# An encoder block on one core: matrix N turned on ACT, outputs at the chain's priority, paired value products, held-back filler, routing order

## The chip, the cores and the metric

One core of a Trainium2 chip runs the whole kernel. The metric is the device time of one execution in microseconds; lower is better. The engines are TensorE (PE, with its weight loads as PEld), VectorE (DVE), ScalarE (ACT), GpSimd (POOL) and SyncE (SP, which issues most transfers).

## The reference

One layer over 2048 tokens of width 1024, in float32. Two token mixers run in parallel on the same normalised input, and a routed channel mixer follows:

```python
h = rms_norm(x, norm_mix_g)
u = h @ w_in                                  # RWKV columns | q, k, v | two gates
y_rwkv = rwkv7_bidir(token_shift(u[..., :RWKV_COLS]), ...)
y_attn = banded_gqa_attention(q, k_att, v_att, attn_sink)   # blocks of 128, window 128
merged = sigmoid(gl_rwkv) * (y_rwkv @ w_proj_rwkv) + sigmoid(gl_attn) * (y_attn @ w_proj_attn)
x = x + merged @ w_out
x = x + expert_choice_moe(rms_norm(x, norm_ffn_g), ...)     # 16 experts take their 256 best tokens each
return rms_norm(x, norm_final_g)

# the RWKV scan, once forwards and once backwards, 8 heads of 64:
s_kk = S @ kk_t
S = S * w_t - outer(s_kk, a_t * kk_t) + outer(v_t, k_t)
y_t = S @ r_t
```

The attention has 8 query heads on 2 key-value heads of 64. The router takes softmax(h @ w_router) and the 256 largest affinities for each expert.

## The kernel before, in words

The kernel runs in stages. First come the normalisation and the RWKV input products (to about 400 us). Then a **prep** (to about 945): 32 iterations of `Prep` build from keys, decays and rates the chunked form of the scan, 64 chunks of C = 32 tokens, with the products for the two gates ("gates", L500, `mm<-h,w`) as filler on TensorE. The chunked form needs, for each chunk and head, the inverse of a triangular 32 x 32 matrix N. `Invert` makes it: it loads N for one direction and one quarter of the sequence, 128 matrices at a time with one matrix in each partition, and solves row after row on DVE: L410 multiplies rows of X by a column of N into `tmp`, L411 sums them. There are eight inversions, three inside the prep and five (`late`) at the start of and inside the next stage, four rows a step.

The **chain** (945 to 1770) is the recurrence: 64 steps, each for both directions (`Chain.step`). A step issues for each direction the products with W (L659, `ps<-W,PRA`), a copy `ur` on ACT, the products with X (L666), four copies into W on ACT (L672), the state products (L679, `ps<-W,KT`) with DVE's scaling (L682) into the next W, and the outputs (L687, `y<-W,PRA`). `Steps` runs the two directions in these four parts, n = 0 to 3. A scheduler turns the program into an order for each engine: an instruction written inside `high_priority(offset=...)` is placed as if it had been written that much earlier, and `issue_after(i)` keeps what is inside behind instruction i. Parts n = 0 to 2 run at the chain's priority, and part n = 3, the outputs, doesn't. Between the parts `fill` issues gates (`GATE_STEP` = 4, 6, 4, 0 of them behind part 0, 1, 2, 3). The attention (`attention`, a generator) is cut into pieces which are issued between steps: scores (L757, L758), softmax, transposes of the probabilities (L789) and the value products (L796), two a key block, one for each key-value head, in different halves of the array. After each four steps a block's outputs are added up into `yacc` (L861) and `finish_rwkv` normalises them (L701 to L711), turns them (L714) and stores them.

**Stage 3** (1792 to 2187) projects, gates, multiplies by w_out (`pm`), and makes for each of 16 token tiles the normalised row h2, the routing logits `plg`, the softmax `aff` (`softmax16`) and `z` (L1096, the tile's row for the output). The **routing** (to 2266) turns the affinities over (`aT`, L1143) and finds each expert's threshold by 30 rounds of counting on DVE (L1162), one for each bit, with small matmuls on TensorE; in the rounds DVE also does `rem` (L1157) for splitting the affinities into parts `r5`, and pieces of the splitting of the first experts' weights (L1314, called `small`). ACT meanwhile copies the first three experts' slices of weights (L1308) and the first part of the affinities (L1154, `r<-aff`). The **experts** (to 3411) fill TensorE.

Of the kernel before, what the change touches and what calls it, by code (L numbers as in the profile page):

```python
# [9 lines left out]
F32 = mybir.dt.float32  # L10
# [3 lines left out]
AF = mybir.ActivationFunctionType  # L14
ALU = mybir.AluOpType
# [4 lines left out]
D = 1024  # L20
# [3 lines left out]
NBLK = T // 128  # L24
HEADS = 8
NPAIR = 4
C = 32
NSTEP = T // C
# [22 lines left out]
GATE_PREP, GATE_STEP = 5, (4, 6, 4, 0)  # L51
# [331 lines left out]
class Invert:  # L383


    def __init__(self, k, d, q):
        self.k, self.d, self.q = k, d, q
        self.i = 0

    def run(self, n):  # L390
        k, d, q, nc = self.k, self.d, self.q, self.k.nc
        if self.i > C:
            return
        if self.i == 0:
            self.N = k.inv.tile([128, C, C], F32, name="N")
            for p in range(NPAIR):
                for e in range(2):
                    r0 = (3 - 2 * e - p % 2) * 32
                    nc.sync.dma_start(self.N[(2 * p + e) * 16:(2 * p + e) * 16 + 16],
                                      k.pra[q][r0:r0 + 32, d, p, e, :, 0:C].rearrange("s u t -> u s t"))  # L400
            self.X = k.inv.tile([128, C, C], F32, name="X")
            self.tmp = k.inv.tile([128, C, C], F32, name="tmp")
            nc.gpsimd.memset(self.X, 0.0)
            nc.gpsimd.memset(self.X.rearrange("p s t -> p (s t)")[:, 0:C * C:C + 1], 1.0)
            self.i = 1
        X, N, tmp = self.X, self.N, self.tmp
        for i in range(self.i, min(C, self.i + n)):
            t, r = (i, slice(0, i)) if d == 0 else (C - 1 - i, slice(C - i, C))
            col = N[:, r, t]
            nc.vector.tensor_mul(tmp[:, :i, :i], X[:, r, r], col[:, None, :].to_broadcast([128, i, i]))  # L410
            nc.vector.tensor_reduce(out=X[:, r, t], in_=tmp[:, :i, :i], op=ALU.add, axis=AX.X)  # L411
        self.i = min(C, self.i + n)
        if self.i == C:
            nc.sync.dma_start(k.xt[d][q].rearrange("p h u s t -> (p h u) s t"), X)
            self.i = C + 1
# [309 lines left out]
def attention(k, b):  # L725
# [3 lines left out]
    nc = k.nc  # L729
    q, bq = divmod(b, 4)  # L730
    lo, hi = max(0, b - 1), min(NBLK, b + 2)
    nk = hi - lo
# [4 lines left out]
    for h in range(2):  # L737
        r = slice(h * 64, h * 64 + 64)
# [42 lines left out]
            nc.vector.tensor_scalar(t, t, den[:, i:i + 1], None, op0=ALU.mult)  # L781
        yield 1
    av = k.ps_a.tile([128, 4, 128], F32, name="pa")
    for c in range(nk):
        pT = k.att.tile([128, 2, 4, 128], F32, name="pT", bufs=3)
        for kv in range(2):
            pt = k.ps_a.tile([128, 4, 128], F32, name="pa")
            for i in range(4):
                nc.tensor.transpose(pt[:, i], sc[kv * 4 + i][:, c * 128:(c + 1) * 128], k.ident)  # L789
            if kv:  # L790
                nc.vector.tensor_copy(pT[:, kv], pt)
            else:
                nc.scalar.activation(pT[:, kv], pt, AF.Copy)
        for kv in range(2):
            rows = slice(kv * 64, kv * 64 + 64)
            nc.tensor.matmul(av[rows], lhsT=vs[:, c, rows], rhs=pT[:, kv], start=(c == 0),  # L796
                             stop=(c == nk - 1), tile_position=(0, kv * 64))
        if c < nk - 1:
            yield 1
    ya = k.att.tile([128, 4, 128], F32, name="yat")  # L800
    nc.scalar.activation(ya, av, AF.Copy)
# [3 lines left out]
class Steps:  # L805
# [17 lines left out]
    def step(self, s, fill):  # L823
        k, nc, tc = self.k, self.k.nc, self.k.tc
        i, j = divmod(s, 4)
        blk = [i, NBLK - 1 - i]
        if j == 0:
            self.y = [k.ps_y.tile([128, NPAIR, 2, 64], F32, name=f"y{d}") for d in range(2)]
            if i >= NBLK // 2:
                self.old = []  # L830
                for d in range(2):
                    self.old.append(k.ln.tile([128, 512], F32, name="yold", bufs=2))
                    nc.sync.dma_start(self.old[d], k.ypart[blk[d]])
        if j % 2 == 0:
            for d in range(2):
                with tc.high_priority(offset=k.chain_lead):
                    self.ch[d].load(2 * i + j // 2 + 1)
        steps = [self.ch[d].step(s, self.y[d]) for d in range(2)]
        for n in range(4):
            with ExitStack() as es:  # L840
                if n < 3:
                    es.enter_context(tc.high_priority(offset=k.chain_lead))
                first, second = self.order, 1 - self.order
                mark = next(steps[first])
                with tc.issue_after(mark):
                    mark = next(steps[second])
            if n < 3:
                self.order = second
            fill(n, mark)
        if j < 3:  # L850
            return
        for d in range(2):
            src = self.y[d].rearrange("p c e i -> p (c e i)")
            acc = self.yp.tile([128, 512], F32, name="yacc")
            if i < NBLK // 2:
                with tc.high_priority(offset=k.chain_lead):
                    nc.scalar.activation(acc, src, AF.Copy)
                nc.scalar.dma_start(k.ypart[blk[d]], acc)
            else:
                with tc.high_priority(offset=k.chain_lead):  # L860
                    nc.vector.tensor_add(acc, src, self.old[d])  # L861
                with tc.high_priority(offset=500):
                    finish_rwkv(k, blk[d], acc)


def token_mixers(k, gates, el):
# [4 lines left out]
    with ExitStack() as es:  # L871
# [121 lines left out]
                    break  # L993

        def between(n, mark):
            gates.run(GATE_STEP[n], after=mark)

        gates.run(GATE_MID)
        for s in range(NSTEP):
# [9 lines left out]
def stage3(k, out):  # L1009
# [3 lines left out]
    with ExitStack() as es:  # L1013
# [11 lines left out]
        for b in ORDER:  # L1025
# [36 lines left out]
            for tt in range(4):  # L1062
# [25 lines left out]
                pl = ps_l.tile([128, NEXP], F32, name="plg")  # L1088
                for i in range(KD):
                    nc.tensor.matmul(pl, lhsT=hT[:, i], rhs=wr[:, i], start=(i == 0), stop=(i == KD - 1))  # L1090
                k.last_exp, last = softmax16(k, xp, pl, k.aff[:, tid], rs)
                nc.scalar.activation(h2, xg, AF.Copy, scale=rs)
                nc.sync.dma_start(k.h2[t0:t0 + 128], h2)
                z = xp.tile([128, D], F32, name="z")
                with tc.issue_after(last):
                    nc.vector.scalar_tensor_tensor(out=z, in0=x, scalar=rs, in1=gz, op0=ALU.mult, op1=ALU.mult)  # L1096
                nc.sync.dma_start(out[t0:t0 + 128], z)


def softmax16(k, pool, lg, out, rs):  # L1100
# [6 lines left out]
    e = pool.tile([128, NEXP], F32, name="sme")  # L1107
    ex = nc.scalar.activation(e, lg, AF.Exp, bias=m, scale=rs, accum_out=s)
    nc.vector.reciprocal(s, s)
    return ex.ins, nc.vector.tensor_scalar(out, e, s, None, op0=ALU.mult).ins  # L1110


def route_constants(k, pool):
# [14 lines left out]
def route(k, rp, small):  # L1128
# [7 lines left out]
    with ExitStack() as e2:  # L1136
# [24 lines left out]
        for bit in range(29, -1, -1):  # L1161
            count = nc.vector.tensor_scalar(junk, aTf, cand.bitcast(F32)[:, 0:1], None, op0=ALU.is_ge, op1=ALU.add,  # L1162
                                            accum_out=cnt)
            with tc.issue_after(count.ins):
                if bit in rest:
                    rest[bit]()
                else:
                    next(small, 0)
# [38 lines left out]
def stage4(k, out):  # L1207
# [3 lines left out]
    with ExitStack() as es:  # L1211
# [117 lines left out]
        xs_n = xt.tile([128, 2, KD, CAP], F32R, name="xs")  # L1329
        for h in range(2):  # L1330
            turn(nxt[2], xs_n, h)
        for _ in small:
            pass
        prev = None
        for n in range(N + 1):
            e, f = divmod(n, KD)
# [221 lines left out]
```

## Time and profile before

| | us |
|---|---|
| median of three runs | 3417.12 (3413.95 to 3420.2) |
| profiled execution, its own time | 3421.18 |
| its span | 3419.2 |
| PE busy in the span | 3115.1 (91%) |
| DVE busy | 2330.7 (68%) |
| ACT busy | 1472.7 (43%) |

The mean granted clock of TensorE is 0.955 of full speed. The busy share is an average over stages: TensorE has hardly a gap in the input products, stage 3 and the experts, and gaps in the prep, the chain and the routing, which is where the change works. All times within the program are microseconds from the start of the span.

### The profile page before, as it was taken

The page shows a single profiled execution, that of the slowest core. Times are in us where ns is not written, and L with a number is a line of the kernel's source. Part 1 is how long each engine was busy: PE and PEld are TensorE (multiplying, and loading weights), DVE is VectorE, ACT ScalarE, POOL GpSimd, SP SyncE. Part 2 cuts the span into 40 slices and gives each one's busy share as a digit, 9 for nine tenths or more (in the row PEclk, how much of TensorE's full clock was granted, in tenths as well). Part 3 has the DMA queues.
Part 4 walks back from the last instruction along what each step waited for, and adds up shares of the span by engine and source line. Part 5 has one row for each costly group of instructions (what it writes and reads, how often), then busy time and mean ns, then how long its engine had stood idle before and what let it go on. Part 6 is the DMA issues. An engine that isn't in the chain of part 4 may idle for free. (4 is left out here: it accounts for less than half of the span.)

```text
span 3419.2 us, 65351 instructions
## 1 busy us (share of the span) xinstructions
PE 3115.1 (91%) x26062; PEld 2575.6 (75%) x26062; DVE 2330.7 (68%) x4902; ACT 1472.7 (43%) x2828; POOL 286.7 (8%) x457
## 2 busy tenths in 40 slices
PE   7999898889878888988969999669999999999998
PEld 6888786667656565565647888559999999999997
DVE  6434679798868887776766666466666666666665
ACT  5111455545425454455553333324444444444443
POOL 0000000000020100010100000001112111121111
PEclk9999899999989998999979999879999999999999
DMA  4212587878787667677766554436666666666663
GB/s 147 83 74 90 179 250 219 250 207 247 215 198 182 165 164 174 169 180 191 201 192 207 197 203 161 148 141 223 229 227 247 244 236 232 224 248 245 234 234 124
DMA packets 464576, 665.16 MB, mean 195 GB/s; under 512 B 162312, under 2 KB 345480, under 8 KB 445968
## 3 DMA queue, kind: packets, MB, share of 16 engines
q1 hardware_dynamic: 387824, 535.14, 51.0%
q10 hardware_dynamic: 58304, 59.79, 5.4%
q0 software_dynamic: 18144, 66.07, 5.1%
q8 instruction: 205, 3.36, 0.4%
q14 instruction: 99, 0.81, 0.1%
HBM read 483.66 MB, written 177.21 MB: 193 GB/s over the span
## 5 line engine op out<-in xcount | busy, mean ns | idle before, releaser
L500 PE MATMUL mm<-h,w 128*128 128x512 f32 x2112 | 619.4, 425 | 28.4 <-ACT ev L524 10.0
L91 PE MATMUL pg<-xs,wg 128*128 128x256 f32 x2048 | 583.6, 285 | 0.0
L92 PE MATMUL pg<-xs,wg 128*128 128x256 f32 x2048 | 582.0, 284 | 0.0
L93 PE MATMUL pg<-xs,wg 128*128 128x256 f32 x2048 | 579.6, 283 | 0.0
L500 PEld LDWEIGHTS mm<-h,w 128*128 128x128 f32 x2112 | 385.6, 197 | 122.0 <-ACT ev L524 11.9
L92 PEld LDWEIGHTS pg<-xs,wg 128*128 128x128 f32 x2048 | 392.4, 192 | 4.6 <-DVE xs L1264 0.2
L91 PEld LDWEIGHTS pg<-xs,wg 128*128 128x128 f32 x2048 | 392.3, 192 | 4.6 <-ACT xs L1263 0.2
L93 PEld LDWEIGHTS pg<-xs,wg 128*128 128x128 f32 x2048 | 392.3, 192 | 0.0
L98 DVE TENSOR_TENSOR wg<-raw,wg 128x2048 fp32r<-128x2048 f32 x125 | 286.3, 2290 | 106.7 <-ACT wg L97 106.5
L97 ACT ACTIVATE w<-wraw 128x1024 fp32r<-128x1024 f32 x135 | 142.6, 1058 | 293.7 <-issue 155.2
L1351 ACT ACTIVATE sg<-pg 128x256 f32<-128x256 f32 x128 | 49.3, 385 | 488.3 <-PE pg L93 486.2
L97 ACT ACTIVATE wg<-raw 128x2048 fp32r<-128x2048 f32 x125 | 238.8, 1910 | 0.1
L410 DVE TENSOR_TENSOR tmp<-X,N 128x1 f32<-128x1 f32 (+30 forms) x248 | 189.2, 763 | 36.9 <-DMA N<-pra 21.1
L83 PE MATMUL mm<-h,w 128*128 128x512 f32 x480 | 189.6, 396 | 20.3 <-ACT w L97 13.0
L92 PE MATMUL py<-wd,hd 128*128 128x512 f32 x512 | 203.1, 397 | 0.0
L91 PE MATMUL py<-wd,hd 128*128 128x512 f32 x512 | 201.0, 393 | 0.0
L93 PE MATMUL py<-wd,hd 128*128 128x512 f32 x512 | 198.4, 390 | 0.0
L98 DVE TENSOR_TENSOR w<-wraw,w 128x1024 fp32r<-128x1024 f32 x135 | 164.7, 1221 | 45.3 <-ACT w L97 44.7
L84 PE MATMUL mm<-h,w 128*128 128x512 f32 x480 | 188.7, 394 | 0.0
L85 PE MATMUL mm<-h,w 128*128 128x512 f32 x480 | 188.4, 393 | 0.0
L1352 DVE TENSOR_TENSOR sg<-pg,sg 128x256 f32<-128x256 f32 x128 | 54.2, 423 | 193.0 <-ACT sg L1351 193.0
L672 ACT ACTIVATE W<-ps 32x128 f32<-32x128 f32 x512 | 137.5, 269 | 70.5 <-PE ps L666 53.1
(302 smaller groups left out, 6243.8 us busy)
## 6 DMA issues: line engine op xcount, KB each, us to landing
raw<-w_exp SPq DMA_DIRECT2D x128, 1536.0 KB, 6.6
wraw<-w_in SPq DMA_DIRECT2D x103, 512.0 KB, 5.1
PRA<-pra SPq DMA_DIRECT2D x64, 512.0 KB, 5.9
pra<-PR SPq DMA_DIRECT2D x64, 256.0 KB, 4.7
pra<-A SPq DMA_DIRECT2D x64, 256.0 KB, 3.8
kt<-KT ACTq DMA_DIRECT2D x128, 128.0 KB, 5.1
gl<-ev ACTq DMA_DIRECT2D x64, 256.0 KB, 4.0
KT<-kt SPq DMA_DIRECT2D x128, 128.0 KB, 5.9
```

What stands on the lines that cost most here:

```text
L83: nc.tensor.matmul(ps, lhsT=w[:, 0, i], rhs=hs[i][:, 0], start=(i == 0), stop=False)
L84: nc.tensor.matmul(ps, lhsT=w[:, 0, i], rhs=hs[i][:, 1], start=False, stop=False)
L85: nc.tensor.matmul(ps, lhsT=w[:, 1, i], rhs=hs[i][:, 0], start=False, stop=(i == KD - 1))
L91: nc.tensor.matmul(out, lhsT=w[0], rhs=x[0], start=start, stop=False)
L92: nc.tensor.matmul(out, lhsT=w[0], rhs=x[1], start=False, stop=False)
L93: return nc.tensor.matmul(out, lhsT=w[1], rhs=x[0], start=False, stop=stop)
L97: nc.scalar.activation(hi, x, AF.Copy)
L98: (eng or nc.vector).tensor_sub(lo, x, hi)
L410: nc.vector.tensor_mul(tmp[:, :i, :i], X[:, r, r], col[:, None, :].to_broadcast([128, i, i]))
L500: nc.tensor.matmul(self.ps, lhsT=w[:, t // 2, i], rhs=h[:, t % 2], start=(self.i == 0), stop=(self.i == 3 * KD - 1))
L672: nc.scalar.activation(W[qd(u), o, e].rearrange("p g i -> p (g i)"), ps[qd(u), 128:256], AF.Copy)
L1352: nc.vector.tensor_mul(sg, pg[:, 1], sg)
```

## The change

Five edits, independent of each other in the code:

```diff
 class Invert:
...
             self.N = k.inv.tile([128, C, C], F32, name="N")
+            self.tmp = k.inv.tile([128, C, C], F32, name="tmp")
...
-                    nc.sync.dma_start(self.N[(2 * p + e) * 16:(2 * p + e) * 16 + 16],
+                    nc.sync.dma_start(self.tmp[(2 * p + e) * 16:(2 * p + e) * 16 + 16],
...
             self.X = k.inv.tile([128, C, C], F32, name="X")
-            self.tmp = k.inv.tile([128, C, C], F32, name="tmp")
+            nc.scalar.activation(self.N, self.tmp.rearrange("p s t -> p t s"), AF.Copy)
...
-            col = N[:, r, t]
+            col = N[:, t, r]
```

N is loaded into `tmp`, ACT copies it transposed into N, and L410 reads a row of that in place of a column.

```diff
     av = k.ps_a.tile([128, 4, 128], F32, name="pa")
-    for c in range(nk):
-        pT = k.att.tile([128, 2, 4, 128], F32, name="pT", bufs=3)
...
-        for kv in range(2):
-            rows = slice(kv * 64, kv * 64 + 64)
-            nc.tensor.matmul(av[rows], lhsT=vs[:, c, rows], rhs=pT[:, kv], start=(c == 0),
-                             stop=(c == nk - 1), tile_position=(0, kv * 64))
-        if c < nk - 1:
+    pTs = []
+    for c in range(nk + 1):
+        if c < nk:
+            pT = k.att.tile([128, 2, 4, 128], F32, name="pT", bufs=3)
...
+            pTs.append(pT)
+        if c:
+            with k.tc.issue_after(mm.ins):
+                for kv in range(2):
+                    rows = slice(kv * 64, kv * 64 + 64)
+                    nc.tensor.matmul(av[rows], lhsT=vs[:, c - 1, rows], rhs=pTs[c - 1][:, kv], start=(c == 1),
+                                     stop=(c == nk), tile_position=(0, kv * 64))
+        if c < nk:
             yield 1
```

The value products of a key block are issued one piece later, behind the next block's transposes.

```diff
             with ExitStack() as es:
-                if n < 3:
-                    es.enter_context(tc.high_priority(offset=k.chain_lead))
+                es.enter_context(tc.high_priority(offset=k.chain_lead))
...
-                with tc.high_priority(offset=500):
+                with tc.high_priority(offset=500 if i + 1 < NBLK else -400):
                     finish_rwkv(k, blk[d], acc)
...
         def between(n, mark):
-            gates.run(GATE_STEP[n], after=mark)
+            gates.run(GATE_STEP[n] if s < NSTEP - 8 else GATE_STEP[n] // 2, after=mark)
```

The outputs get the chain's priority too; in the last eight steps half as many gates are issued (what is left is issued behind the last step), and the last blocks' finishes are placed later.

```diff
-                k.last_exp, last = softmax16(k, xp, pl, k.aff[:, tid], rs)
-                nc.scalar.activation(h2, xg, AF.Copy, scale=rs)
+                k.last_exp = softmax16(k, xp, pl, k.aff[:, tid], rs)
+                with tc.issue_after(k.last_exp):
+                    nc.scalar.activation(h2, xg, AF.Copy, scale=rs)
                 nc.sync.dma_start(k.h2[t0:t0 + 128], h2)
-                z = xp.tile([128, D], F32, name="z")
-                with tc.issue_after(last):
-                    nc.vector.scalar_tensor_tensor(out=z, in0=x, scalar=rs, in1=gz, op0=ALU.mult, op1=ALU.mult)
+                z = xp.tile([128, D], F32, name="z", bufs=2)
+                nc.vector.scalar_tensor_tensor(out=z, in0=x, scalar=rs, in1=gz, op0=ALU.mult, op1=ALU.mult)
...
+            k.last_count = count.ins
...
-        for _ in small:
-            pass
+        with tc.issue_after(k.last_count):
+            for _ in small:
+                pass
```

`z` gets a second buffer and no longer stands behind the softmax, and the pieces of weight splitting that are left over stay behind the last count.

What the scheduler makes of it, at three places. On TensorE in the chain's 37th step of the kernel before, from the last outputs ahead of the state products on. The names with W_8662 are the second direction's, those with W_8640 the first's; 8 state products of each, and outputs of the first behind six gates:

```order
L687 MATMUL y_14759<-W_8662,PRA_14396 32x64 x3
L789 MATMUL pa<-ident,sc 128x128
L687 MATMUL y_14759<-W_8662,PRA_14396 32x64
L789 MATMUL pa<-ident,sc 128x128
L679 MATMUL ps_14788<-W_8640,KT_8644 64x64 x8
L679 MATMUL ps_14799<-W_8662,KT_8666 64x64 x8
L500 MATMUL mm<-h,w 128x512 x6
L687 MATMUL y_14758<-W_8640,PRA_14384 32x64
L789 MATMUL pa<-ident,sc 128x128 x4
```

The same step of the kernel after (W_8665 is the second direction, W_8643 the first):

```order
L689 MATMUL y_14767<-W_8665,PRA_14404 32x64 x8
L689 MATMUL y_14766<-W_8643,PRA_14392 32x64
L681 MATMUL ps_14796<-W_8643,KT_8647 64x64 x8
L681 MATMUL ps_14807<-W_8665,KT_8669 64x64 x3
L689 MATMUL y_14766<-W_8643,PRA_14392 32x64
L681 MATMUL ps_14807<-W_8665,KT_8669 64x64
L689 MATMUL y_14766<-W_8643,PRA_14392 32x64
L681 MATMUL ps_14807<-W_8665,KT_8669 64x64
```

The last state products of the second direction now alternate with outputs of the first, and this alternation goes on to the last state product, with the gates behind it.

On DVE at the start of the routing, before, from the last tile's affinities on:

```order
L1110 TENSOR_SCALAR aff<-sme,sms 128x16
L1096 SCALAR_TENSOR_TENSOR z<-x_22657,rs_22732,gz 128x1024
L1314 TENSOR_TENSOR wg<-raw,wg 128x256 x4
L1314 TENSOR_TENSOR wd<-raw,wd 128x256 x4
L1143 COPY aT<-pr 128x256
L1149 MEMSET cand 128x1
L1162 TENSOR_SCALAR junk,cnt<-aT,cand 128x256
```

And after:

```order
L1102 SCALAR_TENSOR_TENSOR z<-x_22665,rs_22740,gz 128x1024
L1115 RECIPROCAL sms<-sms 128x1
L1116 TENSOR_SCALAR aff<-sme,sms 128x16
L1150 COPY aT<-pr 128x256
L1156 MEMSET cand 128x1
L1169 TENSOR_SCALAR junk,cnt<-aT,cand 128x256
L1322 TENSOR_TENSOR wg<-raw,wg 128x256
```

z has moved ahead of the affinities, and the eight pieces that stood ahead of aT stand behind the last count now.

On ACT at the same place, before, from the last tile's exponentials on:

```order
L1108 ACTIVATE sme,sms<-plg,smx,rs_22732 128x16
L1308 ACTIVATE wg<-raw 128x2048
L1308 ACTIVATE wd<-raw 128x1024
L1154 ACTIVATE r_22835<-aff 128x256
L1308 ACTIVATE wg<-raw 128x2048
L1308 ACTIVATE wd<-raw 128x1024
```

And after:

```order
L1114 ACTIVATE sme,sms<-plg,smx,rs_22740 128x16
L1099 ACTIVATE h_22736<-xg,rs_22740 128x1024
L1316 ACTIVATE wg<-raw 128x2048
L1316 ACTIVATE wd<-raw 128x1024
L1316 ACTIVATE wg<-raw 128x2048
L1316 ACTIVATE wd<-raw 128x1024
L1316 ACTIVATE wg<-raw 128x2048
L1316 ACTIVATE wd<-raw 128x1024
L1161 ACTIVATE r_22843<-aff 128x256
```

The copy of the affinities has moved from behind the first pair of weight copies to behind the third.

## Rows read from the trace of the kernel before

**Rows 1.** Windows by stage: busy us (instructions) of each engine.

```profile
core 0: us, PE busy (x) PEld busy (x) DVE busy (x) ACT busy (x) POOL busy (x), PEclk, DMA share, GB/s
...
400.00:945.00 545.00, 493.29 (x4083) 392.94 (x4082) 462.99 (x921) 290.03 (x640) 5.17 (x8) 0.95 0.77 228
945.00:1770.00 825.00, 707.86 (x9959) 475.66 (x9957) 629.03 (x1547) 407.60 (x1194) 91.48 (x282) 0.93 0.72 177
```

**Rows 2.** Windows inside the prep and at the start of the chain.

```profile
545.00:655.00 110.00, 89.05 (x677) 71.31 (x678) 103.79 (x198) 60.69 (x133) 1.12 (x2) 0.88 0.76 229
655.00:698.00 43.00, 40.79 (x357) 31.63 (x355) 30.08 (x71) 17.15 (x37) 0.00 (x0) 1.00 0.79 226
698.00:754.00 56.00, 47.67 (x392) 38.36 (x391) 55.49 (x103) 27.74 (x61) 0.00 (x0) 0.91 0.72 213
...
829.00:930.00 101.00, 84.97 (x653) 65.02 (x654) 97.82 (x177) 49.42 (x110) 0.09 (x1) 0.92 0.72 213
945.00:1004.00 59.00, 39.47 (x415) 28.43 (x414) 47.57 (x82) 13.81 (x35) 15.98 (x42) 0.83 0.83 198
```

**Rows 3.** Groups of instructions by line, DVE: busy, mean ns, idle before.

```profile
L410 DVE TENSOR_TENSOR tmp<-X,N 128x1 f32<-128x1 f32 (+30 forms) x248 | 189.2, 763 | 36.9 <-DMA N<-pra 21.1 <-DMA kr<-kT 5.1 <-DMA pra<-PR 4.4
```

**Rows 4.** Groups by line and form, DVE, 545 to 946 us.

```profile
L98 DVE TENSOR_TENSOR w<-wraw,w 128x1024 fp32r<-128x1024 f32 x33 | 40.2, 1222 | 7.2 <-ACT w L97 7.2
...
L333 DVE TENSOR_TENSOR PR<-krv,G 128x256 f32<-128x256 f32 x44 | 18.1, 422 | 0.0
...
L410 DVE TENSOR_TENSOR tmp<-X,N 128x961 f32<-128x961 f32 x3 | 5.6, 1862 | 0.0
...
L410 DVE TENSOR_TENSOR tmp<-X,N 128x256 f32<-128x256 f32 x3 | 1.9, 619 | 0.0
```

**Rows 5.** The page's costliest groups: an ACT copy of 1024 elements.

```profile
L97 ACT ACTIVATE w<-wraw 128x1024 fp32r<-128x1024 f32 x135 | 142.6, 1058 | 293.7 <-issue 155.2
```

**Rows 6.** State products (L679): ns min/median/max, first and last start.

```profile
L679 PE MATMUL ps<-W,KT x2016: 219/222/369, 975.8 to 1756.5; 128*64 128x64 f32 x184
```

**Rows 7.** Timeline of PE in the chain: start us, us, engine, line.

```profile
1396.73 1.02 PE L796 MATMUL pa<-pT,vs 128*64 128x512 f32 x2
...
1401.02 2.10 PE L500 MATMUL mm<-h,w 128*128 128x512 f32 x8
...
1462.96 0.43 PE L687 MATMUL y<-W,PRA 128*32 128x64 f32 x16
1463.32 1.15 PE L679 MATMUL ps<-W,KT 128*64 128x64 f32 x32
...
1668.93 1.15 PE L679 MATMUL ps<-W,KT 128*64 128x64 f32 x32
1670.01 0.31 PE L687 MATMUL y<-W,PRA 128*32 128x64 f32 x6
```

**Rows 8.** Timeline of PE between the chain and stage 3.

```profile
1767.11 1.08 PE L796 MATMUL pa<-pT,vs 128*64 128x512 f32 x4
...
1783.47 1.08 PE L714 MATMUL pa<-ident,yacc 128*128 128x128 f32 x4 [13.81 <-DVE yacc L711]
1791.18 1.09 PE L714 MATMUL pa<-ident,yacc 128*128 128x128 f32 x4 [6.63 <-DVE yacc L711]
```

**Rows 9.** Timeline of DVE at the start of the routing.

```profile
2195.58 0.23 DVE L1110 TENSOR_SCALAR aff<-sme,sms 128x16 f32<-128x16 f32 x1
2206.02 1.28 DVE L1096 SCALAR_TENSOR_TENSOR z<-x,rs,gz 128x1024 f32<-128x1024 f32 x1 [10.20 <-DMA out<-z]
2207.22 1.42 DVE L1314 TENSOR_TENSOR wg<-raw,wg 128x256 fp32r<-128x256 f32 x4
...
2209.90 0.42 DVE L1143 COPY aT<-pr 128x256 f32<-128x256 f32 x1
...
2213.08 0.44 DVE L1157 TENSOR_TENSOR rem<-aff,r 128x256 f32<-128x256 f32 x1
```

**Rows 10.** Timeline of ACT at the start of the routing.

```profile
2198.00 0.90 ACT L1154 ACTIVATE r<-aff 128x256 bf16<-128x256 f32 x1
...
2206.55 1.04 ACT L1308 ACTIVATE wd<-raw 128x1024 fp32r<-128x1024 f32 x1
```

More of the change, by code (lines that the diff above doesn't have):

```diff
@@ L783, in attention @@
     av = k.ps_a.tile([128, 4, 128], F32, name="pa")
-    for c in range(nk):
-        pT = k.att.tile([128, 2, 4, 128], F32, name="pT", bufs=3)
-        for kv in range(2):
[L787 to L794, printed above, removed]
-            rows = slice(kv * 64, kv * 64 + 64)
-            nc.tensor.matmul(av[rows], lhsT=vs[:, c, rows], rhs=pT[:, kv], start=(c == 0),
-                             stop=(c == nk - 1), tile_position=(0, kv * 64))
-        if c < nk - 1:
+    pTs = []
[3 more added lines that the diff above has]
+            for kv in range(2):
+                pt = k.ps_a.tile([128, 4, 128], F32, name="pa")
+                for i in range(4):
+                    mm = nc.tensor.transpose(pt[:, i], sc[kv * 4 + i][:, c * 128:(c + 1) * 128], k.ident)
+                if kv:
+                    nc.vector.tensor_copy(pT[:, kv], pt)
+                else:
+                    nc.scalar.activation(pT[:, kv], pt, AF.Copy)
+            pTs.append(pT)
+        if c:
+            with k.tc.issue_after(mm.ins):
+                for kv in range(2):
+                    rows = slice(kv * 64, kv * 64 + 64)
+                    nc.tensor.matmul(av[rows], lhsT=vs[:, c - 1, rows], rhs=pTs[c - 1][:, kv], start=(c == 1),
+                                     stop=(c == nk), tile_position=(0, kv * 64))
+        if c < nk:
             yield 1
@@ L1109, in softmax16 @@
     nc.vector.reciprocal(s, s)
-    return ex.ins, nc.vector.tensor_scalar(out, e, s, None, op0=ALU.mult).ins
+    nc.vector.tensor_scalar(out, e, s, None, op0=ALU.mult)
+    return ex.ins
 def route_constants(k, pool):
```

## Prediction

> **What bounds the kernel now.** I read the busy time by stage first [rows 1]. TensorE is full in the input products, in stage 3 and in the experts; nothing here touches those. In the prep (400 to 945 us) it is busy 493 of 545 us, in the chain (945 to 1770) 708 of 825, so an edit there is worth what it takes out of TensorE's gaps or out of the recurrence, and what it adds to either.
>
> The prep in stretches [rows 2]: between two inversions (655 to 698) TensorE is busy 40.8 of 43 us. In the three stretches with an inversion it idles 110 − 89.0 = 21.0, 56 − 47.7 = 8.3 and 101 − 85.0 = 16.0 us, while DVE is busy 94, 99 and 97%: there DVE sets the pace. The same at the start of the chain (945 to 1004, fourth inversion): TensorE idles 19.5 of 59 us.
>
> In the chain a step takes 12.6 us: the state products (L679) of 63 steps start between 975.8 and 1756.4 us, 62 intervals [rows 6]. It is a recurrence (PRA products, copy, X products, four copies a direction, state products, scaling), so what TensorE puts in front of the last state product counts whole.
>
> **Invert: N turned round on ACT.** The strided multiplication takes 1862 ns for 961 elements and 619 for 256: 1.76 ns an element and 168 fixed [rows 4]. The nearest contiguous multiplication of DVE with two operands, L333, takes 422 ns for 256, and L98 1222 for 1024: 1.04 an element [rows 4]. An inversion multiplies the sum of i² for i up to 31 = 10,416 elements, so 0.72 ns each is 7.5 us, of L410's 189.2 / 8 = 23.7 us [rows 3]; eight give 60 us of DVE. This holds if the stride is the cause. The bounds are 0 and 60.
>
> The Trainium skill, SBUF — State Buffer, Specifications, says SBUF has 16-byte lines and that an access that crosses to a new one pays a penalty; N was read at 128 bytes' stride, and the matched pair of 256 elements, 619 against 422 ns, agrees. [...]
>
> Where it lands: three inversions in the prep save 22.5 us of DVE in stretches where TensorE idles 45; PE, ACT and DMA take over some of it: I take −19 (bounds −10 and −25). At the start of the chain −4 of 7.5, since the load of N is waited for there too. In the chain the four that are left (30 us of DVE) stand in DVE's order beside the scaling that each step waits for; most of it lies beside TensorE's own work: −5 (bounds 0 and −12). The copy costs ACT 1.06 us a time [rows 5], eight times, strided perhaps twice that; in the chain it stands in ACT's order between ur and the W copies, so it is on the recurrence, and it now waits for the load where DVE waited before (21.1 us in three waits, [rows 3]): +2 (bounds 0 and +10). Sum of the edit: **−26**.
>
> **Outputs at the chain's priority.** The listing of the order shows what happens: outputs (L687, 32-column tiles) slide in between the second direction's state products (L679, 64-column tiles), in the most frequent pattern one output ahead of the last state product, in others up to seven one by one; 140 returns over the chain. All changes of tile shape on TensorE go from 675 to 921, those between outputs and state products from 59 to 404. Price: 16 outputs start at 1462.96 and end 0.43 later [rows 7]; one takes 0.22, as a state product does at its shortest [rows 6], so the last starts at 1463.17, and the state products begin at 1463.32: 0.15 us later. The other way: 32 state products from 1668.93, 1.15 long, last start 1669.86, next output 1670.01: 0.15 [rows 7]. In a run the 32 are 0.93 / 31 = 0.03 apart. So a change costs 0.12, 246 more of them **+30 us**, nearly all before the last state product. Bounds: below, 0.12 with half hidden behind the waits for W copies, +15; above, a whole product of 0.22 drained at each of two changes a return, 140 × 0.44 = +62. I take 30.
>
> The Trainium skill, TensorEngine Tiling (Array Packing), Key Properties, says that changing the tiling mode drains the TensorE; it speaks against this edit. The 0.15 against 0.03 agrees with it; were every change a drain of a whole product, the sum would be that of rival (a).
>
> **Value products in pairs.** A lone value product (L796, two instructions in the trace) takes 1.02 us [rows 7], an adjacent pair, four instructions, 1.08 [rows 8]: the second product is nearly free where the two stand side by side. But the order pairs few: 59 lone runs, 12 pairs and 3 triples become 45, 17, 3 and a quad, 77 slots of 1 us become 70. −7; part of it stands in gaps: **−6**.
>
> **Filler.** Gates after step 56 go from 14 a step to 7, the rest to the last step; the total is the same. Eight gates hold TensorE 2.10 us [rows 7], 0.25 each and the end of the last; 37 fewer in six steps: **−9**. In the last step 39 run, 13 ahead of the outputs (3.3 us beside X products and copies that take nearly as long: **+0.5**), the rest while TensorE has nothing to do. That passage hardly changes: after its last value product TensorE waits 13.8 us for DVE's yacc (L711), then 6.6 for the second [rows 8]; the listing still has DVE's chain to the second L711 of the same length and both finishes' transposes ahead of stage 3's first product, so 26 gates in the hole cost nothing and shorten nothing. The −400 offset alone: 0.
>
> **Routing order.** Now DVE has the last affinities at 2195.6 but its next instruction, z, waits 10.2 us for the store of the z before (one buffer), 1.28 long, then eight pieces of weight splitting (1.42 for four), so aT, the input of the 30 counts, is made at 2209.9, and `rem` behind the third count at 2213.1, 3.2 later [rows 9]. After: z has two buffers and is ahead, the eight pieces are behind the counts (2.7 us, only moved), so aT comes near 2198.3. That would be −11.6 + 2.7 = −9. But the listing moves ACT's copy of aff into r5 from behind the first weight pair to behind the third. ACT's third pair ends at 2206.55 + 1.04 = 2207.6 since its raw comes late, and the copy of 0.90 behind it at 2208.5 [rows 10]. DVE's `rem`, in the new listing one count later, is due at 2198.3 + 3.2 + 1.1 = 2202.6, needs that copy and stalls 5.9 us: **−3** (bounds 0 and −9).
>
> **Sum.** −26 + 30 − 6 − 9 + 0.5 − 3 = −13.5, say **−14 us**. Against the profiled execution's own 3421.2 us that is 3407; it lies 4.1 above the median of the three runs, so the same sum against 3417.1 is **3403 us**.
>
> **Rivals.** (a) The mixing costs a whole drain, 0.44 a return: 62 in place of 30 gives +18, **3435 us**, slower. It decides from 30 + 14 = 44 us, 0.31 a return. For it: outputs and state products differ in shape and each lone one must finish; against: the measured 0.15. (b) The stride isn't the price: L410 stays at 23.7 us an inversion, the edit is +2 in place of −26, total +14: **3431 us**, slower. Against it stands the matched pair in [rows 4]; for it that X is read in short rows too, which no contiguous row shows. (c) The switches hide behind the W copies (+15), the raw lands early so routing gains its 9, the DVE gain comes whole (22.5 + 7.5 + 12 in place of 28): 14 + 15 + 6 + 14 = 49 less, **3368 us**; half of what it adds, 3386, is likelier. (d) No net change: the saved DVE time is not TensorE's in the prep (ACT or the loads bound it there at 10 us less gain), about **3413 us**.
>
> **How the numbers follow.** Forecast (3393 to 3411) 0.46, (a) 0.16, (b) 0.06, (c) 0.18, (d) 0.14. A measurement here tells 0.2%, 6.8 us, from no change: faster is below 3410.3. Faster: 0.42 of the forecast's 0.46, and (c), 0.60; slower: (a) and (b) without their near part, 0.21; same: the rest, 0.19. Range 3380 to 3433: it leaves out the better end of (c) and the worse of (a), 1 in 10 each. The forecast alone: 3393 to 3411.
>
> **What the next profile shows.** Right: L410 near 16 us an inversion (mean 520 ns) and TensorE idle in the prep down by some 19; steps of the chain 0.1 to 0.3 us longer outside inversions and state products taking 1.5 us or more where they were 1.15; z free of its store and a stall before `rem`. Wrong: L410 unchanged; C blocks lengthened by over 1 us a step; the chain shorter than 825 us in spite of 921 changes of shape; TensorE starting the experts more than 6 us sooner after the affinities.

## The result and the profile after

The changed kernel takes 3434.9 us (median of 4 runs) against 3415.5 for the kernel before: a ratio of 1.0063, 95% interval 1.0047 to 1.0078, so slower by some 20 us (19 by the medians, 21 by the ratio). The forecast was 3403, faster.

Busy time by stage, as in [rows 1]:

```profile
400.00:945.00 545.00, 498.63 (x4106) 398.67 (x4107) 438.00 (x922) 296.94 (x649) 5.23 (x8) 0.94 0.79 230
945.00:1770.00 825.00, 733.35 (x9857) 497.98 (x9856) 586.96 (x1530) 410.57 (x1182) 87.81 (x282) 0.93 0.72 173
```

DVE is relieved in both stages (463 to 438, 629 to 587 us), and TensorE is busier in the chain (708 to 733 us) with about as many instructions (9959 and 9857). The group that answers to [rows 3]:

```profile
L412 DVE TENSOR_TENSOR tmp<-X,N 128x1 f32<-128x1 f32 (+30 forms) x248 | 126.3, 509 | 31.2 <-ACT N L404 20.8 <-DMA wraw<-w_in 5.2 <-issue 1.1
```

And the forms of [rows 4]:

```profile
L412 DVE TENSOR_TENSOR tmp<-X,N 128x961 f32<-128x961 f32 x3 | 3.5, 1162 | 0.0
...
L412 DVE TENSOR_TENSOR tmp<-X,N 128x256 f32<-128x256 f32 x3 | 1.3, 425 | 0.0
```

L410's 189.2 us are 126.3, and the form with 256 elements takes 425 ns, as L333 did (422): the stride was the whole difference, 63 us of DVE where 60 were forecast. But the multiplication, which waited 21.1 us for the load [rows 3], now waits 20.8 us for ACT's copy.

Where the time went, by the first instruction of each stage in the two traces (us from the span's start; the distance to the line above is the stage):

| | before | after | stage, after − before |
|---|---|---|---|
| chain's first product (L659, L661) | 962.5 | 957.3 | −5.3 |
| chain's last output | 1766.4 | 1772.4 | +11.3 |
| stage 3's first product | 1791.9 | 1803.8 | +5.9 |
| last affinities (DVE) | 2195.6 | 2223.0 | +15.5 |
| experts' first product | 2264.9 | 2285.4 | −7.0 |
| end of the span | 3419.2 | 3438.9 | −0.7 |

Each column is one execution, and whole executions of the kernel before lie between 3402 and 3421 us, so a few us in a stage may be noise. The forecast's terms for the chain add up to some +8 us, near the 11.3 by luck, since single terms are off by more (below). It is off ahead of the chain (−19 for the prep alone), in the passage from the chain to stage 3 (0), and in stage 3, for which it has no term. The end of stage 3 on ACT:

```profile
2205.36 0.60 ACT L1086 ACTIVATE hT<-pt 128x512 f32<-128x512 f32 x1 [0.20 <-PE pt L1085]
2217.99 1.06 ACT L1090 ACTIVATE h<-x 128x1024 f32<-128x1024 f32 x1 [12.03 <-DMA h<-h]
```

And on SP's queue, ahead of it:

```profile
2200.48 0.81 SPq L1276 DMA_DIRECT2D raw<-w_exp  x2
2201.39 0.38 SPq L1087 DMA_DIRECT2D x<-x  x1
2201.81 0.78 SPq L1276 DMA_DIRECT2D raw<-w_exp  x1
2202.63 0.45 SPq L1100 DMA_DIRECT2D h<-h  x1
```

The last tile's Square (L1090) writes its unused squares into h2's only buffer, and waits 12.03 us for the store of the tile before. That store stands on SP's queue behind three loads of 1.5 MB, because h2's copy is now held behind the exponentials. In [rows 9] z waited 10.2 us for such a store, but after the affinities were made; this wait is ahead of them. And the stall forecast for `rem` is there on DVE, 3.3 us and not 6, since everything ahead of it is later:

```profile
2223.00 0.23 DVE L1116 TENSOR_SCALAR aff<-sme,sms 128x16 f32<-128x16 f32 x1
2223.85 0.42 DVE L1150 COPY aT<-pr 128x256 f32<-128x256 f32 x1 [0.62 <-PE pr L1149]
...
2232.29 0.44 DVE L1164 TENSOR_TENSOR rem<-aff,r 128x256 f32<-128x256 f32 x1 [3.32 <-ACT r L1161]
```

In the chain the outputs mix with the state products as the order said; TensorE in the 43rd step:

```profile
1516.83 1.03 PE L681 MATMUL ps<-W,KT 128*64 128x64 f32 x26
1517.79 0.30 PE L689 MATMUL y<-W,PRA 128*32 128x64 f32 x2
1518.02 0.33 PE L681 MATMUL ps<-W,KT 128*64 128x64 f32 x2
1518.27 0.30 PE L689 MATMUL y<-W,PRA 128*32 128x64 f32 x2
1518.50 0.33 PE L681 MATMUL ps<-W,KT 128*64 128x64 f32 x2
```

From one start to the next it is 0.23 to 0.25 us for two instructions. Over the 63 blocks of state products of the kernel that has this edit alone, the time from the first to the last start is 0.95 us without a change of shape inside (17 blocks), 1.45 with two (25), 1.79 with four, 2.27 with six, 3.13 with ten, 4.36 with sixteen: a slope of 0.21 us a change, 0.42 a return. That is rival (a)'s price, not the forecast's 0.12. (The moved output's own time is in it.)

### The profile page after: what moved, and what is told of

It reads as the page before. It is cut to its first block, busy times and chain, and to the rows that moved or that the text cites. A ratio compares the mean times of both kernels' runs of the same rounds, so it can differ in the third digit from the quotient of the medians.

```text
span 3438.9 us, 65310 instructions
## 1 busy us (share of the span) xinstructions
PE 3161.5 (92%) x26062; PEld 2615.7 (76%) x26062; DVE 2269.8 (66%) x4902; ACT 1484.4 (43%) x2836; POOL 283.8 (8%) x457
## 5 line engine op out<-in xcount | busy, mean ns | idle before, releaser
L84 PE MATMUL mm<-h,w 128*128 128x512 f32 x480 | 189.2, 395 | 0.0
L98 DVE TENSOR_TENSOR wd<-raw,wd 128x1024 fp32r<-128x1024 f32 x125 | 152.4, 1219 | 2.3 <-ACT wd L97 2.3
```

Source lines behind the costliest of these rows:

```text
L84: nc.tensor.matmul(ps, lhsT=w[:, 0, i], rhs=hs[i][:, 1], start=False, stop=False)
L98: (eng or nc.vector).tensor_sub(lo, x, hi)
```

## The experiments

All ratios are to the kernel before, run beside it on the same chip; 0.1% is 3.4 us.

| run | what it is | median us | ratio, 95% interval |
|---|---|---|---|
| e_inv | Invert alone | 3412.1 | 0.9997 (0.9986 to 1.0009) |
| e_outs | outputs' priority alone | 3443.6 | 1.0095 (1.0076 to 1.0114) |
| e_pairs | value products alone | 3411.6 | 0.9994 (0.9982 to 1.0005) |
| e_fill | filler alone, with the later last finishes | 3412.3 | 0.9999 (0.9988 to 1.0010) |
| e_route | routing edits alone | 3420.9 | 1.0023 (1.0011 to 1.0036) |
| a_sqz | changed, Square into z | 3423.8 | 1.0034 (1.0021 to 1.0047) |
| e_route_h2f | routing alone, h2 not held | 3405.2 | 0.9983 (0.9971 to 0.9996) |
| a_nomix | changed, outputs unmixed | 3430.3 | 1.0050 (1.0037 to 1.0063) |
| c_nomix_sqz | both of these | 3423.3 | 1.0028 (1.0017 to 1.0039) |
| a_noouts | changed, no outputs' priority | 3402.2 | 0.9983 (0.9968 to 0.9997) |
| e_inv_pool | Invert alone, copy on POOL | 3377.3 | 0.9904 (0.9886 to 0.9923) |
| e_inv_late | Invert alone, copy a step later | 3396.2 | 0.9961 (0.9948 to 0.9973) |
| p_outs | e_inv_pool and outputs' priority | 3407.6 | 0.9980 (0.9970 to 0.9991) |
| c_best2 | changed, no outputs' priority, h2 not held | 3393.3 | 0.9947 (0.9929 to 0.9964) |
| c_best3 | the same, copy on POOL | 3390.1 | 0.9941 (0.9928 to 0.9954) |
| a_pool_h2f | c_best3 with outputs' priority | 3385.1 | 0.9936 (0.9916 to 0.9955) |
| c_min | e_inv_pool and e_route_h2f | 3369.5 | 0.9875 (0.9855 to 0.9895) |

**The five edits one by one.** Each is its part of the change's diff, on the kernel before; of each one or two lines that matter (the marks behind # are added here):

```diff
+            nc.scalar.activation(self.N, self.tmp.rearrange("p s t -> p t s"), AF.Copy)   # e_inv
...
-                if n < 3:                                                                   # e_outs
...
+    for c in range(nk + 1):                                                                 # e_pairs
...
+            gates.run(GATE_STEP[n] if s < NSTEP - 8 else GATE_STEP[n] // 2, after=mark)     # e_fill
...
+                with tc.issue_after(k.last_exp):                                            # e_route
```

> The kernel before with the Invert edit alone (N turned round by an ACT copy). Theory L (the ledger of the two traces: prep 5 us shorter, then the chain's start 2 us, the rest of the change's gain in the chain hidden by the mixing): 8 to 18 us faster than before, L410 at 126 us in all. Rival R (the ACT copies of 2 us and the changed order cost in the chain what DVE saves; the mixing of outputs is hidden): within 5 us of before or slower.

> The kernel before with the outputs at the chain's priority alone. Theory L: changes of tile shape in the chain go from 675 to 950 at 0.12 us each, nearly all before the last state product, so 25 to 35 us slower, all of it between steps 8 and 63. Rival R (the changes hide behind waits for the W copies): within 8 us of before.

> The kernel before with the value products one piece later alone. 77 runs of value products become 69: both theories 0 to 8 us faster. More than that says that lone value products cost the recurrence more than their own 1 us.

> The kernel before with the filler edit alone (half the gates in the last eight steps, the last finishes placed later). Theory L: steps 57 to 63 shorter by 6 to 9 us, and the passage to stage 3 longer by about 6 us since the gates that were held back stand there and the finish comes later: within 4 us of before. Rival F (the passage's holes take the gates for nothing, as forecast): 6 to 10 us faster.

> The kernel before with the routing edits alone (z in two buffers, h2's copy behind the exponentials, the left pieces behind the last count). Theory L: the store of tile 15's h2 is issued behind three loads of 1.5 MB and the last tile's Square, which writes into the same buffer, waits about 12 us for it, so the last affinities come 11 to 15 us later; then 7 us less to the experts: 3 to 9 us slower. Rival R (that wait comes from the later start of stage 3 in the full change and not from these edits): 5 to 9 us faster.

Invert: no difference, which is rival R's number but not its reason: in the two traces the chain starts 9.3 us sooner than before and is 4.9 us shorter, and stage 3 is some 8 us longer (411.2 us to the last affinities in place of 403.7), which no theory has. Outputs: 32 us slower, theory L's number, by another sum than L's (below). Pairs and filler: no difference that can be told. Routing: 8 us slower, with the last affinities 415.1 us after stage 3's first product where it was 403.7, then 62.4 to the experts where it was 69.4. Alone, the five make about +37 us; together +21, so they don't add; all but the routing change one order, that of the chain.

**Routing: whose wait.** Two ways out of h2's wait. In the changed kernel:

```diff
-                nc.scalar.activation(h2, x, AF.Square, accum_out=ss)
+                z = xp.tile([128, D], F32, name="z", bufs=2)
+                nc.scalar.activation(z, x, AF.Square, accum_out=ss)
```

> The changed kernel with the Square of stage 3 writing its unused squares into z's buffer in place of h2's, so that no Square waits for h2's store. Theory L: the last affinities come 11 us sooner and the stall before rem goes (3 us): 11 to 16 us faster than the changed kernel, 3 to 9 slower than before. Rival Q (the queue behind the three weight loads is the cost, and another transfer takes the place of h2's store): within 4 us of the changed kernel.

And in the routing edits alone:

```diff
-                with tc.issue_after(k.last_exp):
-                    nc.scalar.activation(h2, xg, AF.Copy, scale=rs)
+                nc.scalar.activation(h2, xg, AF.Copy, scale=rs)
```

> The kernel before with the routing edits except one: h2's copy isn't held behind the exponentials, so that tile 15's h2 is stored ahead of the three weight loads. Theory L (that hold alone makes the last Square wait): the wait of 12 us is gone, aT is made within 3 us of the last affinities, rem doesn't stall, 5 to 10 us faster than before. Rival Q (with the hold gone another buffer's release comes last, as in the run with the Square in z's buffer, where aT waited 10 us for the h2 copy): within 3 us of before.

The first takes 10 us off the changed kernel, a little under the expected 11 to 16: the affinities come 1.2 us after the last logits product, but the scheduler then puts h2's copy behind all weight copies on ACT, and aT, which waits for it, comes 10 us later. On DVE:

```profile
2200.34 0.23 DVE L1116 TENSOR_SCALAR aff<-sme,sms 128x16 f32<-128x16 f32 x1
2210.58 0.42 DVE L1150 COPY aT<-pr 128x256 f32<-128x256 f32 x1 [10.01 <-ACT h L1100]
```

So rival Q was right on the mechanism (another wait takes the place), and L nearly on the time. The second removes the hold alone and turns the routing edits from +8 into −6 us: the hold is worth 14 us, and is the cause of the slower stage 3 (400.5 us to the affinities). Even there aT waits, now for a store of x that stands behind two of the weight loads:

```profile
2192.32 0.42 DVE L1143 COPY aT<-pr 128x256 f32<-128x256 f32 x1 [5.93 <-DMA x<-x]
```

**Outputs: the mixing or the place.** First the changed kernel with outputs not mixed, and that with the Square in z:

```diff
                 es.enter_context(tc.high_priority(offset=k.chain_lead))
+                if n == 3:
+                    es.enter_context(tc.issue_after(mark))
```

> The changed kernel, with the outputs at the chain's priority held behind the second direction's last state product, so that none stands between two state products. Changes between outputs and state products go from 404 to 63, all changes of tile shape from 921 to 514 (675 before the change). Theory L (each change costs 0.12 us on the recurrence): 407 x 0.12 = 49 us less at most, 25 to 45 faster than the changed kernel, so 5 to 25 faster than the kernel before. Rival P (it is the outputs' place ahead of filler and value products, not the mixing, that lengthens the steps): within 8 us of the changed kernel, 12 to 28 slower than before.

> The changed kernel with both mendings, outputs not mixed into the state products and the Square in z's buffer. Theory L: the gains add, 36 to 60 us faster than the changed kernel and 16 to 40 faster than the kernel before. Rivals P and Q: 0 to 12 faster than the changed kernel, slower than before.

Only some 4 us less than the changed kernel, and with the Square in z 2 us less than a_sqz: theory L's expectation failed, and rival P's number came true. TensorE is busy 270 us in 325 of the steps 31 to 56, where the changed kernel has 293 in 326; but the steps are no shorter. The blocks of state products are short again (1.06 us from the first to the last start in place of 1.71), but the next W is ready 2.83 us behind the last of them in place of 2.10, and the rest of the step is the same to 0.1 us. What TensorE waits for there, unmixed:

```profile
PE ps L668 <- ACT ur L664: 23.4, 7, 5.4
```

The changed kernel waits 7.7 us for ur in these steps. ACT stands in order behind a transfer for another block's finish, with ur behind it:

```profile
1506.30 1.50 ACT L720 ACTIVATE yt<-pa,vec 128x128 f32<-128x128 f32 x4 [4.27 <-DMA yr<-yt]
1507.68 0.85 ACT L751 ACTIVATE kh<-kr 128x768 fp32r<-128x768 f32 x1
1508.42 0.45 ACT L664 ACTIVATE ur<-ps 128x128 f32<-128x128 f32 x2
```

So the unmixing moved ACT's order too; that this one place stands for the seven such waits is read from the trace, not tested. Since the part of the step with ur in it is no longer than in the changed kernel, this wait isn't where the gain went: it went behind the last state product. TensorE's mean granted clock is lower too, 0.91 in these steps in place of 0.95; what that costs wasn't measured. Whether the outputs cost by the mixing (L) or by their place (P), this run doesn't tell. Taking the edit back measures both together:

```diff
-                es.enter_context(tc.high_priority(offset=k.chain_lead))
+                if n < 3:
+                    es.enter_context(tc.high_priority(offset=k.chain_lead))
```

> The changed kernel with the outputs' priority taken back (part 3 of a step without the chain's priority, as before the change). Theory L (the outputs' priority costs what it cost alone, 32 us): 20 to 34 us faster than the changed kernel, so 0 to 12 faster than before. Rival M (the other edits fill the same gaps, so in the full change it costs little, as the run with unmixed outputs suggested): within 10 us of the changed kernel, 11 or more slower than before.

0.8%, 27 us, less than the changed kernel, as L said of the whole edit; the chain from first product to last output is 782 us where it was 815.

**Invert: what eats DVE's 63 us.** The copy on another engine, and on ACT a step later:

```diff
-            nc.scalar.activation(self.N, self.tmp.rearrange("p s t -> p t s"), AF.Copy)
+            nc.gpsimd.tensor_copy(self.N, self.tmp.rearrange("p s t -> p t s"))
```

```diff
-            nc.scalar.activation(self.N, self.tmp.rearrange("p s t -> p t s"), AF.Copy)
+            self.wait = 4 if n == 1 else 1      # 4 calls in the prep, 1 in the chain
...
             self.i = 1
+            return
+        if self.wait:
+            self.wait -= 1
+            if self.wait:
+                return
+            nc.scalar.activation(self.N, self.tmp.rearrange("p s t -> p t s"), AF.Copy)
```

> The kernel before with the Invert edit, the transposing copy on POOL in place of ACT. Theory G (the copy's 2 us on ACT, eight times, and the waits behind it eat what DVE gives): 6 to 14 us faster than before. Rival H (the time that DVE saves isn't on the path except in the prep, and what the prep gains is lost at the start of stage 3): within 4 us of the run with the copy on ACT, so within 5 of before.

> The kernel before with the Invert edit, the copy on ACT, but written one step (in the prep four calls) after the load, so that the data has landed when ACT comes to it. Theory G1 (ACT standing in order behind the load's landing is the cost): most of what the copy on POOL gains, 18 to 32 us faster than before. Theory G2 (the copy's 2 us in ACT's order, in front of the copies that a step waits for, are the cost): within 8 us of the run with the plain edit, so 0 to 9 faster than before.

On POOL the same edit is worth 33 us in place of 1, over twice what G expected. Between the two profiled executions, 35 us apart, 8.5 us lie ahead of the chain, 14.0 in it, 1.9 in the passage and 9.6 in stage 3, which copies no N and whose part stays unexplained. POOL's copies take no less than ACT's (the profile's spans on POOL are rough). e_inv's eight copies, min, median and max in ns:

```profile
L404 ACT ACTIVATE N<-tmp x8: 1936/1988/2127, 536.0 to 1306.4; 128x1024 f32<-128x1024 f32 x8
```

And e_inv_pool's:

```profile
L404 POOL COPY N<-tmp x8: 1965/2004/2957, 531.0 to 1313.1; 128x1024 f32<-128x1024 f32 x8
```

What differs is who stands behind the copy. e_inv in the chain, ACT:

```profile
1197.80 0.50 ACT L664 ACTIVATE ur<-ps 128x128 f32<-128x128 f32 x2 [0.89 <-PE ps L661]
1205.65 1.94 ACT L404 ACTIVATE N<-tmp 128x1024 f32<-128x1024 f32 x1 [7.35 <-DMA kr<-kT]
1207.61 1.14 ACT L674 ACTIVATE W<-ps 32x128 f32<-32x128 f32 x4
```

and TensorE at the same place:

```profile
1198.99 0.65 PE L668 MATMUL ps<-ur,X 32*32 32x64 f32 x32
...
1207.93 1.31 PE L689 MATMUL y<-W,PRA 128*32 128x64 f32 x16 [6.50 <-ACT W L674]
```

The X products are done at 1199.6, but the W copies, in order behind the copy of N and its wait of 7.35 us, begin at 1207.6: the recurrence stands for 8 us. (The profile names kr's load, the next on the queue; N's own load landed at 1205.3.) The prep has the same: in e_inv ACT waits 6.52 us for the load at 793 to 800, with the next sigmoid inputs behind it, and so in the changed kernel:

```profile
794.82 0.84 ACT L295 ACTIVATE th<-pl,vec 128x256 f32<-128x256 f32 x2
803.20 1.94 ACT L404 ACTIVATE N<-tmp 128x1024 f32<-128x1024 f32 x1 [7.53 <-DMA tmp<-pra]
805.04 0.61 ACT L314 ACTIVATE th<-th 128x512 f32<-128x512 f32 x1
```

Issued later (e_inv_late), the copy finds its load landed in the prep, where the same copy waits for nothing. This run gains 13 of POOL's 33 us: the chain starts at 940.6, where six kernels with the old Invert start between 962.5 and 967, seven with the copy on ACT between 952.8 and 957.4 and five with the copy on POOL between 944.8 and 949.3. So in the prep G1 holds: the wait seen there, some 7 us, is about what the chain's start gains with POOL, 8 us, and half of what it gains with the late copy, 15; the other half wasn't followed. In the chain the edit didn't do what it was written for. Its second copy there:

```profile
1110.36 0.44 ACT L670 ACTIVATE ur<-ps 128x128 f32<-128x128 f32 x2
1120.71 1.94 ACT L413 ACTIVATE N<-tmp 128x1024 f32<-128x1024 f32 x1 [9.90 <-DMA pT<-qt]
1122.55 0.58 ACT L801 ACTIVATE pT<-pa 128x512 f32<-128x512 f32 x1
1123.15 2.31 ACT L680 ACTIVATE W<-ps 32x128 f32<-32x128 f32 x8
```

N's load landed at 1120.6, so the copy still stands in wait for it, ahead of the W copies. The four copies in the chain wait 18.3 us in all, 11.5 in e_inv, and the chain takes 802 us to the last output, 799 in e_inv, 785 with POOL. So for the chain this run separates G1 from G2 no better than e_inv does, and the 13 us, between G1's 18 to 32 and G2's 0 to 9, settle neither.

**Do they add?** p_outs puts the outputs' edit on e_inv_pool; the others combine edits shown above, as the table says:

```diff
-                if n < 3:
-                    es.enter_context(tc.high_priority(offset=k.chain_lead))
+                es.enter_context(tc.high_priority(offset=k.chain_lead))
```

> The kernel before with the Invert edit (copy on POOL) and the outputs at the chain's priority. Changes of tile shape go from 665 to 878. Theory L (each return between outputs and state products costs about 0.42 us on the recurrence): 22 to 34 us slower than the run without the outputs' edit, so 0 to 12 us faster than before. Rival M (with DVE and ACT relieved the returns hide, as the pair of runs with all other edits suggested): within 10 us of the run without, so 23 or more faster than before.

> The changed kernel without the outputs' priority and without the hold on h2's copy: Invert, pairs, filler and the rest of the routing edits. Theory L: -1 (Invert), -2 (pairs), 0 (filler), -8 (routing), 6 to 16 us faster than before. Rival M: slower than before, since the steps are longer for another reason than the outputs.

> The changed kernel with three mendings: outputs without the chain's priority, h2's copy not held, and N's transposing copy on POOL. Theory L+G (the gains add: 18 us of the version without the outputs' priority and the hold, and some 25 to 32 of the copy's move): 38 to 52 us faster than before. Rival S (the gain of the copy's move was a lucky order of that one kernel): 12 to 25 us faster.

> The changed kernel with the outputs' priority kept, h2's copy not held, and N's copy on POOL. Theory L+G: it differs from the kernel with all three mendings by the outputs' cost alone, 25 to 34 us: 8 to 24 us faster than before. Rival M (the outputs' priority costs little once ACT is out of the way): within 10 us of the kernel with all three mendings.

> The kernel before with two edits alone: Invert with N's copy on POOL, and the routing edits without the hold on h2's copy. TensorE's order in the chain is that of the run with the Invert edit and POOL alone. If gains in different stages add: 33 + 6 = 36 to 42 us faster than before. If the start of the experts or stage 3 takes some back: 28 to 35.

p_outs is 26 us slower than e_inv_pool, by the outputs alone, with the slope of 0.21 us a change again: L. c_best2 is 18 us faster than before, a little over its expectation. c_best3 is no better than it (2 us, within the intervals), as S said: POOL starts the chain 7 us sooner again, but the 14 us that it was worth inside the chain in e_inv_pool are not there (797 us, 795 in c_best2). And a_pool_h2f, which keeps the outputs' priority, is as fast as c_best3: against L, for M, in this pair alone. What the outputs' priority adds to the chain in the four pairs of traces (one execution each), summed over 62 steps, in us:

| without, with | state products, first to last start | from there to the next W's end | rest of the step | sum |
|---|---|---|---|---|
| before, e_outs | +52 | −33 | +3 | +23 |
| a_noouts, after | +59 | −34 | +10 | +36 |
| e_inv_pool, p_outs | +40 | −37 | +17 | +20 |
| c_best3, a_pool_h2f | +43 | −37 | −10 | −5 |

In all four the mixing lengthens the blocks by 40 to 59 us, and 33 to 37 of it come back behind them, so that it costs 3 to 26 us on balance. What makes the fourth pair differ is the rest of the step (W products, ur, X products, W copies), whose order is another in each kernel. The chain's mean granted clock is another too, 0.91 in c_best3 and 0.95 in a_pool_h2f, 0.92 and 0.95 in e_inv_pool and p_outs. Neither the order nor the clock was tried by itself, so why the fourth pair costs nothing stays open. c_min leaves TensorE's order of the chain as e_inv_pool has it and mends the routing, in another stage: 43 us faster than before, where the two alone make 39. It is the fastest run.

## Why the prediction was wrong

**What bounds the kernel; L410's stride.** Right: DVE was relieved by 63 us (60 forecast), and the gain of 19 taken for the prep is what the edit gives where ACT doesn't wait in order for the load: the chain starts 17 us sooner with the copy on POOL (mean of five) and 24 with the late copy, against 964.8, the mean of the six starts with the old Invert. The penalty for each access that crosses to a new 16-byte line (the Trainium skill, SBUF — State Buffer, Specifications) agrees with 425 ns at 256 elements in place of 619.

**The step that failed first:** "The copy costs ACT 1.06 us a time … it now waits for the load where DVE waited before (21.1 us in three waits, [rows 3]): +2 (bounds 0 and +10)". A copy of 2.0 us was taken for 1.06 to 2, which is not the error. The error is that the wait for the landing was counted as moved from DVE to ACT at the same price. It wasn't moved but doubled: DVE waits 20.8 us for the copy where it waited 21.1 for the load, and ACT waits 11.4 us for the load besides, with the prep's th and ta, ur and the W copies in order behind it. The forecast had 19 us of gain in the prep; the changed kernel starts its chain 5.3 us sooner, and the seven kernels with the copy on ACT 9 us sooner on average: 8 us less than with POOL, 15 less than with the late copy. In the chain the price stays open: its four copies wait 3.9 us in the changed kernel and 11.5 in e_inv, and the move to POOL takes 14 us off the chain in one pair of kernels and none in the other. The 32 us between e_inv and e_inv_pool are thus the price in that one pair, stage 3's 9.6 included; between c_best2 and c_best3 it is 2.

**The step that failed second:** "That would be −11.6 + 2.7 = −9 … −3 (bounds 0 and −9)". From the affinities on it held: 62.4 us to the experts in place of 69.4. But SP's queue was not followed for h2's store, which the hold moves behind the three loads, and no term looked at what is behind that store: the last Square and with it the affinities. Measured +8 in place of −3, and −6 with that hold taken out.

**Outputs, +30:** measured +32 alone, 27 in the changed kernel, 26 and none in the two other pairs. The sum was right by luck, by two errors that cancel: a change costs 0.21 us, not 0.12 (the first start after a change was measured against the last start of a run, which hides that the next product of the same kind is late as well), and over half is given back behind the last state product, where the outputs stood: in e_outs the blocks last 1.83 us in place of 0.96 in steps 31 to 56, but W's end follows 1.83 in place of 2.50 us behind the last one. The 0.21 agrees with the rule that changing the tiling mode drains TensorE (the Trainium skill, TensorEngine Tiling (Array Packing), Key Properties).

**Pairs −6 and filler −8.5:** −2 and 0, intervals −6 to +2 and −4 to +3. Fewer gates in a step shorten it only if TensorE is what the step waits for; in e_fill steps 57 to 62 take 12.2 us in place of 12.6 with half the gates. The passage, forecast unchanged, is no longer with either alone (filler 24.7, pairs 21.4 us from last output to stage 3's first product, 25.6 before) but takes 31.4 in the changed kernel. It is 27 to 31 us in the five kernels that have pairs, filler and the outputs' priority, and 23 to 24 in the three with pairs and filler alone; why was not followed.

**The rivals.** The measured time is (a)'s 3435 us, but not by (a): its price per return was right, but its sum leaves out what comes back behind the blocks. Rival (d) had the prep nearly right: it let ACT or the loads bound it, with 10 us less gain, and 10 to 14 are missing there. The wait for h2's store, worth 14 us, was in no rival.

## What to carry to other kernels

A wait that is moved to another engine costs what is queued behind it there: before moving work, list the next instructions of the new engine and who waits for them, and give the work to an engine with nothing behind it (POOL here) or issue it after the data has landed, and look in the trace whether it has. When a copy is held back, follow its store along the queue to the next writer of the same buffer. Judge an edit that changes a scheduler's order by taking it out of the finished kernel as well as by adding it alone, since neither sum is additive.

## What the runs showed of the hardware

A change between products in 32-column and in 64-column tiles cost 0.21 us on TensorE in four kernels (the changed one, e_outs, p_outs, a_pool_h2f), for runs as short as two instructions. A transposing copy of 1024 fp32 elements a partition takes 1.99 us on ACT and 2.00 on POOL (roughly), where a contiguous one takes 1.06 on ACT ([rows 5]): there the stride costs a factor of 1.9, on DVE's multiplication 1.6 at 961 elements.
